# Gates and branch products of an encoder block computed with tokens on the partitions

## The chip, the cores and the metric

The kernel runs on one NeuronCore of a Trainium2 chip. The metric is device time in microseconds of one execution, taken as the median over several runs. The engines have short names in the profile: PE is TensorE with its matmuls, PEld its loading of the stationary operand, DVE is VectorE, ACT is ScalarE, POOL is GpSimd, SP is SyncE, which only issues DMAs here.

## What is computed

One layer of a bidirectional encoder on 256 tokens with 2048 features. The input is normed and projected by `w_in`; two attention branches (8 heads in a window, 12 dilated heads whose three groups merge to 4) give `ya` and `yb`; each is projected to 2048 features, multiplied with its gate and summed; an output projection, a gated MLP with a width-3 convolution over the tokens, and a gated embedding follow.

```python
for i in range(DEPTH):
    h = rms_norm(x, attn_norm[i])
    proj = h @ w_in[i]
    qa, ka, va, qb, kb, vb, ga, gb = jnp.split(proj, split_points, axis=-1)
    ya = windowed_gqa(qa, ka, va, rel_bias_table, sink_a[i])
    yb = dilated_attention(qb, kb, vb, rel_bias_table)
    merged = jax.nn.sigmoid(ga) * (ya @ w_branch_a[i]) + jax.nn.sigmoid(gb) * (yb @ w_branch_b[i])
    x = x + merged @ w_out[i]
    hf = rms_norm(x, ffn_norm[i])
    g = dwconv_centred(hf @ w_ffn_gate[i], conv_w[i], conv_b[i])
    x = x + (jax.nn.gelu(g) * (hf @ w_ffn_up[i])) @ w_ffn_down[i]
    gate_p = jax.nn.sigmoid(rms_norm(x, ple_norm[i]) @ w_ple_gate[i])
    x = x + gate_p * (p[i] @ w_ple_proj[i])
return rms_norm(x, final_norm)
```

The widths that matter: D_MODEL 2048 (16 blocks of 128), `ya` 1024 wide (8 blocks), `yb` 512 wide (4 blocks), the MLP 5632 wide (44 blocks). All inputs are float32.

## The kernel before

**Work.** All weights are cut into blocks of 128x128 and laid out in HBM in the order of use, in pieces of 16 blocks (1 MB). There are 4128 blocks. SyncE loads the pieces in turn into three buffers (`raw`, line 176). Every float32 operand is split into a high part that TensorE reads in one pass and the low rest: for each eight blocks, ScalarE copies the high part (`whi`, line 192) and VectorE subtracts it from the original (`wlo`, line 193). `split_to` issues that up to three groups of eight ahead; there are four buffers of each. A product is then high x high + high x low + low x high.

**Jobs.** `_plan` makes a list of jobs; the main loop (line 674 on) goes through it, and TensorE's instructions stand in that order. There are two forms.

- A *product job* (`product`, `block`) makes one output block of 128 features x 256 tokens, features on the partitions. Per weight block: the high weights are stationary and 512 columns move (256 tokens high, 256 tokens low, line 203); then the low weights are stationary and the 256 high columns move (line 204). `gather` adds the two 256-column halves of the accumulator (ScalarE line 254, VectorE line 258). The kinds are q, k, ga, gb, ba, bb, g and u.
- A *wide job* (`wide_product`) makes 256 tokens x 512 features, tokens on the partitions, in two accumulators of 128 tokens. Per step of four weight blocks and per half of the tokens, three matmuls of 512 columns: token block high with high weights, token block high with low weights, token block low with high weights (lines 226 to 228). The token block is stationary and the weights move. The kinds are v, o, d0, d1, pp and pg. Two of the v jobs take every second token (`TWINS`, a stationary operand with a step of two columns), for the dilated heads; the others take unbroken halves.

Each job of 16 blocks (a product job) or 64 blocks (a wide one over 2048 features) is followed by what other engines do with the result (`after`, `joined`, `gate`). Other pieces of work are put into the stream by `at((job, step), f)`: `run_due` calls f just before that step of that job. The last attention head group is handled so: scores one job later at step 9, the transposes of the softmax two jobs later at step 12, the product with the values three jobs later at step 4 (`attend`).

**The stage in question.** Job numbers 38 to 101 are ga n, gb n (gates, 16 blocks each, moving operand `hs`, the gained input) and ba n, bb n (branch products, 8 and 4 blocks, moving operand `yab`), for n = 0 to 15: 704 blocks. ga and gb are multiplied with the norm's factor and go through tanh (lines 574 to 577); a sigmoid is (tanh of half + 1)/2. ba and bb multiply (lines 580 to 588), and `halves` writes block n of `merged`, high and low part, features on the partitions, as o needs it for its stationary operand. In job o the tokens stand on the partitions; `joined` adds the residual `res`, and `flip` turns four columns of 128 back by four transposes on TensorE per call (line 618). `res` lies in the place of `x`, whose rows are fetched again from HBM by eight DMAs on ScalarE's queue (`fetch`, line 662), during ga 2 to ga 9.

**Places in SBUF.** The pools give every tile a fixed byte address per partition. Modulo 512, all `whi` and `wlo` buffers and both buffers named `mov` (which hold `hs`, then `merged`, `hf`, `pl`) are at 160; `yab` is at 0; `act` (the stationary operand of d0 and d1) and `pw` (that of pp) are at 96. The rows and halves inside these tiles are multiples of 512 bytes.

Of the kernel before, what the change touches and what calls it, by code (L numbers as in the profile page):

```python
# [10 lines left out]
F32 = mybir.dt.float32  # L11
# [5 lines left out]
P = 128  # L17
# [44 lines left out]
def _plan():  # L62
# [25 lines left out]
    lead = 2  # L88
    for n in range(KC + lead):
        if n < KC:  # L90
            jobs.append(("ga", n, "w_in", GA + n, 0, KC))
            jobs.append(("gb", n, "w_in", GB + n, 0, KC))
        if n >= lead:
            jobs.append(("ba", n - lead, "w_branch_a", n - lead, 0, QH))
            jobs.append(("bb", n - lead, "w_branch_b", n - lead, 0, HG))
    def wide(kind, name, k0, count):
        for c in range(QUARTERS):
            jobs.append((kind, c, name, tuple(range(4 * c, 4 * c + 4)), k0, count))

    wide("o", "w_out", 0, KC)  # L100
# [35 lines left out]
def _encoder(ctx: ExitStack, tc, xt, xrows, pt, cols, table, onehot, mask, ident_in, last_gain, wts, out):  # L136
# [187 lines left out]
    def at(i, f, *a):  # L324

        due.setdefault(i, []).append((f, a))
# [8 lines left out]
    yab = ap_.tile([P, QH + HG, 2 * T], FR, name="yab", bufs=1)  # L335
# [184 lines left out]
    def after(job, i, acc, u=None):  # L520
# [52 lines left out]
        elif kind in ("ga", "gb"):  # L573
            u = gather(acc)
            nc.vector.tensor_tensor(u, u, rt[0], op=ALU.mult)
            g = ap_.tile([P, T], F32, name="th", tag="k", bufs=7)
            nc.scalar.activation(g, u, AF.Tanh, scale=0.5)
            tg[kind, n] = g
        elif kind == "ba":
            u = gather(acc)  # L580
            m = ap_.tile([P, T], F32, name="ma", tag="q", bufs=4)
            nc.vector.scalar_tensor_tensor(m, tg.pop(("ga", n)), 1.0, u, op0=ALU.add, op1=ALU.mult)
            held["ma"] = m
        elif kind == "bb":
            u = gather(acc)
            m = ap_.tile([P, T], F32, name="mb", tag="q", bufs=4)
            nc.vector.scalar_tensor_tensor(m, tg.pop(("gb", n)), 1.0, u, op0=ALU.add, op1=ALU.mult)
            nc.vector.tensor_tensor(m, m, held["ma"], op=ALU.add)
            halves(held["merged"][:, n, :], m)
# [71 lines left out]
    def fetch(t, c):  # L661
# [3 lines left out]
        "q": lambda k: hs[:, k, :], "ba": lambda k: yab[:, k, :], "bb": lambda k: yab[:, QH + k, :],  # L665
        "g": lambda k: held["hf"][:, k, :],
    }
    for a in ("k", "ga", "gb"):
        movers[a] = movers["q"]
    movers["u"] = movers["g"]  # L670

    stills = {"o": "merged", "d0": "act", "d1": "act", "pp": "ps", "pg": "pl"}

    for i, job in enumerate(_JOBS):
        kind, n, _, _, _, blocks = job
        if kind == "ba" and n == 0:
# [22 lines left out]
        if kind == "ga" and 2 <= n < 10:  # L699
            at((i, 4), fetch, *divmod(n - 2, QUARTERS))  # L700
# [7 lines left out]
        if kind == "pp" and n == 2:  # L708
            half = held["half"] = held["ff"].tile([P, 2], F32, name="half")
            nc.vector.tensor_scalar(half, root(rowsums(held["ss2"]), 2), 0.5, None, op0=ALU.mult)  # L710
# [43 lines left out]
def _layout(inputs):  # L754
# [18 lines left out]
    for g, (window, dil) in enumerate(PATTERNS):  # L773
# [3 lines left out]
        "xt": xt, "xrows": np.asarray(inputs["x"])[0].reshape(2, P, D), "pt": pt, "cols": cols,  # L777
        "table": np.asarray(inputs["rel_bias_table"]), "onehot": onehot, "mask": mask, "ident": np.eye(P, dtype=f),
        "last_gain": np.broadcast_to(np.asarray(inputs["final_norm"]), (P, D)), "wts": wts.reshape(_NPIECES, P, PIECE * P),
    }  # L780
# [18 lines left out]
```

## Time and profile before

| | |
|---|---|
| median of 3 runs | 1500.01 us (1499.2 to 1501.3) |
| the profiled execution | 1501.29 us, span 1499.5 us |
| granted TensorE clock over the span | 0.996 |
| instructions in the trace | 20395, of them 7936 matmuls |
| read from HBM | 279.49 MB |

The span runs from the first to the last instruction of the profiled execution; the execution's own time has 1.8 us more around it. Busy times are shares of the span. Matmuls overlap each other in the trace (the next begins while the one before drains), so the mean duration of a matmul is longer than the distance between two of them; the distance is found from a stretch's length and the number of blocks in it. A view named "windows" gives such stretches. A line of the waits has the waiting engine and line, who released it, the time in total, the number of waits and the longest.

### The profile page before, as it was taken

The page shows a single profiled execution, that of the slowest core. Times are in us where ns is not written, and L with a number is a line of the kernel's source. Part 1 is how long each engine was busy: PE and PEld are TensorE (multiplying, and loading weights), DVE is VectorE, ACT ScalarE, POOL GpSimd, SP SyncE. Part 2 cuts the span into 40 slices and gives each one's busy share as a digit, 9 for nine tenths or more (in the row PEclk, how much of TensorE's full clock was granted, in tenths as well). Part 3 has the DMA queues.
Part 4 walks back from the last instruction along what each step waited for, and adds up shares of the span by engine and source line. Part 5 has one row for each costly group of instructions (what it writes and reads, how often), then busy time and mean ns, then how long its engine had stood idle before and what let it go on. Part 6 is the DMA issues. An engine that isn't in the chain of part 4 may idle for free.

```text
span 1499.5 us, 20395 instructions
## 1 busy us (share of the span) xinstructions
PE 1483.9 (99%) x7936; PEld 1276.7 (85%) x7936; DVE 1015.7 (68%) x1533; ACT 748.9 (50%) x1119; POOL 3.7 (0%) x9
## 2 busy tenths in 40 slices
PE   9999999999999999999999999999999999999997
PEld 8888888888888888888888888888888888888886
DVE  6596665666676675578888885447887877555565
ACT  6465444445555555555555554334554554444553
POOL 0000000000000000000000000000000000000000
PEclk9999999999999999999999999999999999999999
DMA  8744444445555554555554455444544545454452
GB/s 302 278 169 159 169 169 172 173 165 193 196 182 186 196 189 184 195 202 191 197 193 180 190 196 196 186 185 191 196 176 190 187 180 195 186 181 195 184 189 104
DMA packets 46380, 282.94 MB, mean 189 GB/s; under 512 B 5124, under 2 KB 9988, under 8 KB 14028
## 3 DMA queue, kind: packets, MB, share of 16 engines
q1 hardware_dynamic: 44268, 277.31, 50.0%
q10 hardware_dynamic: 2016, 4.33, 0.9%
q8 instruction: 62, 1.02, 0.3%
q14 instruction: 34, 0.28, 0.0%
HBM read 279.49 MB, written 2.14 MB: 188 GB/s over the span
## 4 chain that ended last, share of the span: by engine, by line
PE 95%; DMA 3%; DVE 1%; ACT 1%; issue 0%; SPq 0%; POOL 0%; POOLq 0%; DVEq 0%; ACTq 0%
PE acc L203 39%; PE acc L204 20%; PE acc L226 11%; PE acc L227 11%; PE acc L228 11%; DMA raw<-in_wts 2%; DMA x<-in_xrows 1%; PE pt L482 0%; PE pt L618 0%; DVE wlo L193 0%; PE misc L497 0%; PE sp L447 0%; PE misc L428 0%; PE misc L429 0%; PE misc L430 0%
## 5 line engine op out<-in xcount | busy, mean ns | idle before, releaser
L193 DVE TENSOR_TENSOR wlo<-raw,whi 128x1024 fp32r<-128x1024 f32 (+1 forms) x519 | 632.1, 1218 | 442.6 <-ACT whi L192 442.1
L192 ACT ACTIVATE whi<-raw 128x1024 fp32r<-128x1024 f32 (+1 forms) x519 | 547.7, 1056 | 666.5 <-PE acc L203 270.8
L203 PE MATMUL acc<-mov,whi 128*128 128x512 f32 x2352 | 826.5, 395 | 0.0
L204 PE MATMUL acc<-mov,wlo 128*128 128x256 f32 x2352 | 658.9, 280 | 0.0
L203 PEld LDWEIGHTS acc<-mov,whi 128*128 128x128 f32 x2352 | 440.8, 187 | 100.9
L204 PEld LDWEIGHTS acc<-mov,wlo 128*128 128x128 f32 x2352 | 444.3, 189 | 0.5
L226 PE MATMUL acc<-whi,mov 128*128 128x512 f32 (+1 forms) x384 | 148.6, 387 | 3.6 <-DVE first L258 3.6
L228 PE MATMUL acc<-whi,mov 128*128 128x512 f32 (+1 forms) x384 | 147.7, 385 | 0.0
L227 PE MATMUL acc<-wlo,mov 128*128 128x512 f32 (+1 forms) x384 | 147.6, 384 | 0.0
L226 PE MATMUL acc<-whi,act 128*128 128x512 f32 x352 | 138.6, 394 | 0.0
L227 PE MATMUL acc<-wlo,act 128*128 128x512 f32 x352 | 138.4, 393 | 0.0
L228 PE MATMUL acc<-whi,act 128*128 128x512 f32 x352 | 136.8, 389 | 0.0
L226 PEld LDWEIGHTS acc<-whi,mov 128*128 128x128 f32 x384 | 73.9, 193 | 18.0 <-DVE first L258 4.5
L228 PEld LDWEIGHTS acc<-whi,mov 128*128 128x128 f32 x384 | 73.8, 192 | 14.1
L227 PEld LDWEIGHTS acc<-wlo,mov 128*128 128x128 f32 x384 | 73.9, 192 | 13.2
L226 PEld LDWEIGHTS acc<-whi,act 128*128 128x128 f32 x352 | 66.1, 188 | 14.9
L228 PEld LDWEIGHTS acc<-whi,act 128*128 128x128 f32 x352 | 66.1, 188 | 14.9
L227 PEld LDWEIGHTS acc<-wlo,act 128*128 128x128 f32 x352 | 66.2, 188 | 13.1
L254 ACT ACTIVATE t<-acc 128x256 f32<-128x256 f32 x179 | 65.1, 368 | 8.9 <-PE acc L204 8.9
L203 PE MATMUL acc<-yab,whi 128*128 128x512 f32 x192 | 68.4, 395 | 0.0
L258 DVE TENSOR_TENSOR u<-acc,t 128x256 f32<-128x256 f32 x164 | 67.8, 417 | 0.0
L204 PE MATMUL acc<-yab,wlo 128*128 128x256 f32 x192 | 53.9, 280 | 0.0
(140 smaller groups left out, 906.5 us busy)
## 6 DMA issues: line engine op xcount, KB each, us to landing
raw<-in_wts SPq DMA_DIRECT2D x251, 1024.0 KB, 4.8
raw<-in_wts SPq DMA_DIRECT2D x12, 512.0 KB, 6.7
x<-in_xrows ACTq DMA_DIRECT2D x8, 256.0 KB, 6.5
x<-in_xt SPq DMA_DIRECT2D x13, 128.0 KB, 5.3
mov<-hold SPq DMA_DIRECT2D x3, 514.0 KB, 6.9
mov<-hold SPq DMA_DIRECT2D x2, 768.0 KB, 7.8
mov<-in_last_gain ACTq DMA_DIRECT2D x1, 1024.0 KB, 5.0
out<-x ACTq DMA_DIRECT2D x2, 384.0 KB, 3.5
```

The lines of the kernel that those rows point to most:

```text
L192: nc.scalar.activation(hi, src, AF.Copy)
L193: nc.vector.tensor_tensor(lo, src, hi.bitcast(F32), op=ALU.subtract)
L203: nc.tensor.matmul(acc, hi[:, o, :], m, start=first, stop=False, skip_group_check=True)
L204: nc.tensor.matmul(acc[:, T:], lo[:, o, :], m[:, :T], start=False, stop=last, skip_group_check=True)
L226: nc.tensor.matmul(acc, xh, hi, start=(k == 0), stop=False)
L227: nc.tensor.matmul(acc, xh, lo, start=False, stop=False)
L228: nc.tensor.matmul(acc, xl, hi, start=False, stop=(k == n - 1))
L254: keep(nc.scalar.activation(t, acc[:, T:], AF.Copy, scale=scale))
L258: nc.vector.tensor_tensor(u, acc[:, :T], t, op=ALU.add)
```

## The change

The stage ga, gb, ba, bb becomes wide jobs: for each quarter c of the output features the jobs ga c, gb c (64 blocks each), ba c (32) and bb c (16) follow each other. `hs` and the two parts of `yab` are now stationary, and the accumulators hold tokens on the partitions. ScalarE takes tanh straight from the accumulator with the norm's factor as its scale per partition; VectorE multiplies and adds from the accumulators (`gated`). The sum m of a quarter, 256 tokens x 512 features, is then turned by eight transposes on TensorE in two groups of four (`merge`), at steps 3 and 6 of the job after bb, which is the next ga, or o 0 for the last quarter. ScalarE and VectorE write the high and low part of `merged` from there. TensorE has 1056 matmuls of 512 columns and 32 transposes in this stage in place of 704 of 512 and 704 of 256 columns.

The last head's scores, transposes and value product move to steps 3, 8 and 11 of job ga 0. The eight fetches of the residual's rows move to step 6 of each ga and gb. The rows are declared after the weights among the kernel's inputs.

Places: `yab` gets 128 columns more and begins 160 bytes into its tile. The three tiles of row sums and the tile of half the norm's factor become one tile (`marks`). By this `yab`, `act` and `pw` all begin at 160 modulo 512.

```diff
-    lead = 2
-    for n in range(KC + lead):
-        if n < KC:
-            jobs.append(("ga", n, "w_in", GA + n, 0, KC))
-            jobs.append(("gb", n, "w_in", GB + n, 0, KC))
-        if n >= lead:
-            jobs.append(("ba", n - lead, "w_branch_a", n - lead, 0, QH))
-            jobs.append(("bb", n - lead, "w_branch_b", n - lead, 0, HG))
-    def wide(kind, name, k0, count):
-        for c in range(QUARTERS):
-            jobs.append((kind, c, name, tuple(range(4 * c, 4 * c + 4)), k0, count))
-
+    def wide(kind, name, k0, count, first=0, quarters=range(QUARTERS)):
+        for c in quarters:
+            n = first + 4 * c
+            jobs.append((kind, c, name, tuple(range(n, n + 4)), k0, count))
+
+    for c in range(QUARTERS):
+        wide("ga", "w_in", 0, KC, GA, [c])
+        wide("gb", "w_in", 0, KC, GB, [c])
+        wide("ba", "w_branch_a", 0, QH, 0, [c])
+        wide("bb", "w_branch_b", 0, HG, 0, [c])
...
-def _encoder(ctx: ExitStack, tc, xt, xrows, pt, cols, table, onehot, mask, ident_in, last_gain, wts, out):
+def _encoder(ctx: ExitStack, tc, xt, pt, cols, table, onehot, mask, ident_in, last_gain, wts, xrows, out):
...
-    yab = ap_.tile([P, QH + HG, 2 * T], FR, name="yab", bufs=1)
+    yab = ap_.tile([P, (QH + HG) * 2 * T + P], FR, name="yab", bufs=1)
+    yab = yab[:, 40:40 + (QH + HG) * 2 * T].rearrange("p (k t) -> p k t", t=2 * T)
...
-                at((i + 3, 4), values, w, heads, y)
-            at((i + 2, 11 if len(heads) == 1 else 12), second)
-        at((i + 1, 9), first)
+                at((i + 1, 11) if end else (i + 3, 4), values, w, heads, y)
+            at((i + 1, 8) if end else (i + 2, 11 if len(heads) == 1 else 12), second)
+        end = y == QH + HG - 1
+        at((i + 1, 3 if end else 9), first)
...
+    def gated(kind, n, t, acc):
+
+        th, m = held["th"], held["m"][:, t, :]
+        if kind in ("ga", "gb"):
+            nc.scalar.activation(th[:, kind == "gb", t, :], acc, AF.Tanh, scale=held["rc"][:, t:t + 1])
+        elif kind == "ba":
+            nc.vector.scalar_tensor_tensor(m, th[:, 0, t, :], 1.0, acc, op0=ALU.add, op1=ALU.mult)
+        else:
+            u = th[:, 1, t, :]
+            nc.vector.scalar_tensor_tensor(u, u, 1.0, acc, op0=ALU.add, op1=ALU.mult)
+            nc.vector.tensor_tensor(m, m, u, op=ALU.add)
+
+    def merge(n, e, m):
+
+        p = ps.tile([P, 2, T], F32, name="pt", bufs=2)
+        for c in range(2):
+            for t in range(2):
+                nc.tensor.transpose(p[:, c, t * P:(t + 1) * P], m[:, t, (2 * e + c) * P:(2 * e + c + 1) * P], ident)
+        k = 4 * n + 2 * e
+        hi, lo = (held["merged"][:, k:k + 2, c:c + T] for c in (0, T))
+        nc.scalar.activation(hi, p, AF.Copy)
+        nc.vector.tensor_tensor(lo, p, hi.bitcast(F32), op=ALU.subtract)
...
+    held.update(hs=hs, ya=yab[:, :QH, :], yb=yab[:, QH:, :])
+    stills = {"ga": "hs", "gb": "hs", "ba": "ya", "bb": "yb", "o": "merged", "d0": "act", "d1": "act", "pp": "ps", "pg": "pl"}
...
+        if kind == "ga" and n == 0:
+            held["rc"] = sc.tile([P, 2], F32, name="sum")
+            nc.vector.tensor_scalar(held["rc"], rc[0][:, :2], 0.5, None, op0=ALU.mult)
+        if kind == "gb" and n == 0:
...
-            for a in ("ss1", "ss2", "ss3"):
-                held[a] = ff.tile([P, 2, QUARTERS], F32, name=a)
+            marks = ff.tile([P, 5, 2, QUARTERS], F32, name="marks")
+            for e, a in enumerate(("ss1", "ss2", "ss3")):
+                held[a] = marks[:, e]
+            held["half"] = marks[:, 3, 0, :2]
...
-        if kind == "ga" and 2 <= n < 10:
-            at((i, 4), fetch, *divmod(n - 2, QUARTERS))
+        if kind in ("ga", "gb"):
+            at((i, 6), fetch, int(kind == "gb"), n)
+        if kind == "bb":
+            for e in range(2):
+                at((i + 1, 3 + 3 * e), merge, n, e, held["m"])
...
-            tag = ("pt" if kind == "pg" and n % 2 == 0 else "acc" if kind == "pg" else ("acc", "sp")[n % 2])
+            tag = ("pt" if kind == "pg" and n % 2 == 0 else "acc" if kind == "pg" else ("acc", "sp")[kind in ("gb", "bb") or kind not in ("ga", "ba") and n % 2])
...
+        elif kind in ("ga", "gb", "ba", "bb"):
+            if kind == "ga":
+                held["th"] = ap_.tile([P, 2, 2, W4], F32, name="th", tag="v", bufs=1)
+                held["m"] = ap_.tile([P, 2, W4], F32, name="m", tag="vf", bufs=1)
+            for t in range(2):
+                if t:
+                    rest()
+                gated(kind, n, t, acc[t])
```

More of the change, by code (lines that the diff above doesn't have):

```diff
@@ L572, in after @@
                 attend(i, [(QH + g * HG + j, KVH + g * HG + j) for g in range(NG)], QH + j)
[L573 to L589, printed above, removed]
         elif kind == "g":
@@ L664, in _encoder @@
     movers = {
-        "q": lambda k: hs[:, k, :], "ba": lambda k: yab[:, k, :], "bb": lambda k: yab[:, QH + k, :],
-        "g": lambda k: held["hf"][:, k, :],
-    }
-    for a in ("k", "ga", "gb"):
-        movers[a] = movers["q"]
+        "q": lambda k: hs[:, k, :], "g": lambda k: held["hf"][:, k, :],
+    }
+    movers["k"] = movers["q"]
     movers["u"] = movers["g"]
-    stills = {"o": "merged", "d0": "act", "d1": "act", "pp": "ps", "pg": "pl"}
+    held.update(hs=hs, ya=yab[:, :QH, :], yb=yab[:, QH:, :])
+    stills = {"ga": "hs", "gb": "hs", "ba": "ya", "bb": "yb", "o": "merged", "d0": "act", "d1": "act", "pp": "ps", "pg": "pl"}
     for i, job in enumerate(_JOBS):
         kind, n, _, _, _, blocks = job
-        if kind == "ba" and n == 0:
+        if kind == "ga" and n == 0:
+            held["rc"] = sc.tile([P, 2], F32, name="sum")
+            nc.vector.tensor_scalar(held["rc"], rc[0][:, :2], 0.5, None, op0=ALU.mult)
+        if kind == "gb" and n == 0:
             held["merged"] = big.tile([P, KC, 2 * T], FR, name="mov")
@@ L708, in _encoder @@
         if kind == "pp" and n == 2:
-            half = held["half"] = held["ff"].tile([P, 2], F32, name="half")
-            nc.vector.tensor_scalar(half, root(rowsums(held["ss2"]), 2), 0.5, None, op0=ALU.mult)
+            nc.vector.tensor_scalar(held["half"], root(rowsums(held["ss2"]), 2), 0.5, None, op0=ALU.mult)
         if i < FIRST:
@@ L776, in _layout @@
     return {
-        "xt": xt, "xrows": np.asarray(inputs["x"])[0].reshape(2, P, D), "pt": pt, "cols": cols,
+        "xt": xt, "pt": pt, "cols": cols,
         "table": np.asarray(inputs["rel_bias_table"]), "onehot": onehot, "mask": mask, "ident": np.eye(P, dtype=f),
         "last_gain": np.broadcast_to(np.asarray(inputs["final_norm"]), (P, D)), "wts": wts.reshape(_NPIECES, P, PIECE * P),
+        "xrows": np.asarray(inputs["x"])[0].reshape(2, P, D),
     }
```

## The prediction

> **What bounds the kernel now.** I read the page's busy shares and chain first, then TensorE's waits, then a table by stage. The page:
>
> ```profile
> PE 1483.9 (99%) x7936; PEld 1276.7 (85%) x7936; DVE 1015.7 (68%) x1533; ACT 748.9 (50%) x1119; POOL 3.7 (0%) x9
> PEclk9999999999999999999999999999999999999999
> PE 95%; DMA 3%; DVE 1%; ACT 1%; issue 0%; SPq 0%; POOL 0%; POOLq 0%; DVEq 0%; ACTq 0%
> ```
>
> TensorE is busy for 99% of the span at full clock and is 95% of the chain that ended last. The view of its waits adds up to under 6 us:
>
> ```profile
> PE acc L226 <- DVE first L258: 3.6, 1, 3.6
> PE misc L159 <- DVE mhalf L154: 1.1, 1, 1.1
> PE first L203 <- DVE mov L271: 0.9, 1, 0.9
> PE first L203 <- ACT whi L192: 0.2, 1, 0.2
> ```
>
> All of it lies in the start; behind it no other engine holds TensorE up. So the change can pay only by the number of matmuls and by the pace at which they follow each other. The pace is read from stretches that begin and end with a job (columns: stretch, its length, busy time and instructions of TensorE, then the same of the others, granted clock, DMA share, GB/s):
>
> ```profile
> core 0: us, PE busy (x) PEld busy (x) DVE busy (x) ACT busy (x) POOL busy (x), PEclk, DMA share, GB/s
> 153.83:178.01 24.18, 24.18 (x119) 20.34 (x118) 14.90 (x19) 10.96 (x15) 0.00 (x0) 1.00 0.44 153
> 235.22:257.62 22.40, 22.40 (x98) 18.53 (x97) 10.77 (x10) 9.26 (x10) 0.00 (x0) 1.00 0.48 169
> 312.48:349.98 37.50, 37.50 (x231) 33.30 (x229) 24.13 (x34) 18.75 (x30) 0.00 (x0) 1.00 0.45 168
> 349.98:562.08 212.10, 212.10 (x1218) 186.07 (x1217) 145.28 (x220) 112.24 (x176) 0.00 (x0) 1.00 0.51 188
> 562.08:583.88 21.80, 21.80 (x98) 18.03 (x97) 13.15 (x18) 9.97 (x13) 0.00 (x0) 1.00 0.54 205
> 583.88:606.64 22.76, 22.76 (x106) 18.80 (x104) 12.78 (x15) 11.47 (x16) 0.00 (x0) 1.00 0.49 177
> 664.64:897.62 232.98, 232.98 (x1347) 205.43 (x1346) 192.59 (x343) 120.60 (x191) 0.00 (x0) 1.00 0.53 192
> 897.62:1018.46 120.84, 120.84 (x531) 99.14 (x529) 59.71 (x57) 47.22 (x46) 0.00 (x0) 1.00 0.50 190
> 1024.10:1267.18 243.08, 243.08 (x1378) 210.82 (x1377) 195.95 (x346) 122.77 (x194) 0.00 (x0) 1.00 0.50 186
> 1402.63:1467.90 65.27, 65.27 (x290) 54.04 (x289) 36.86 (x37) 31.73 (x39) 0.00 (x0) 1.00 0.53 195
> ```
>
> (Two or three matmuls under way at an edge are counted too.) I divide each by its weight blocks of 128x128. Both forms stream 768 columns a block: a product job 512+256, a wide job six matmuls of 512 for four blocks.
> - Product jobs: u 0 to u 21 (664.64 on, 42 jobs of 16 blocks) 232.98/672 = 346.7 ns a block; g 23 to u 43 (1024.10 on, 43 jobs) 243.08/688 = 353.3 ns. Same lines, same tiles: two paces.
> - Wide jobs: pg 0 to 2 (1402.63 on) 65.27/192 = 340.0 ns; o 0 (562.08) 21.80/64 = 340.6; d0 (897.62) 120.84/352 = 343.3; the fourth v job (235.22), whose stationary takes every second column, 22.40/64 = 350.0.
>
> The kernel's pools put the weight halves and both mov tiles (hs, merged, hf, pl) at bytes that are 160 modulo 512; act, d0's stationary, is at 96. That is the one difference I find between 340.0 and 343.3.
>
> **The change, part by part.** I sum on the profiled execution: span 1499.5 us, time 1501.3 with 1.8 us around it, 1.3 us over the median of 1500.0. What is saved I take from the median.
>
> *The gate stage* (ga, gb, ba, bb) now takes 37.50 + 212.10 = 249.6 us for 704 blocks, with 36 matmuls of the last attention head in its first 37.5 us: 37.50 - 96 x 0.3467 = 4.2 us for those. Afterwards the 704 blocks are wide jobs. With hs and yab at 160 modulo 512, I take pg's 340.0 ns: 239.4 us. Bounds: 340.0 (pg) and 350.0 (the fourth v job), 7.0 us apart. I take the low end since o and pg have the same shape and place, and since the third v job (153.83), which reads the same hs as unbroken 128 columns, is 24.18 us with 20 foreign matmuls inside; at 350.0 its 64 blocks would be 22.4 and leave 1.8 us, under the 0.11 to 0.12 us each that such ones take below. The head's 36 matmuls stay: 4.2.
>
> *Added:* 32 transposes in groups of four. The o jobs hold the same thing: o 1 with eight transposes is 22.76 against 21.80 for o 0, so 0.96 us per quarter; three fall into the stage, one into o 0: 3.8 us. Stage and o 0: 239.4 + 4.2 + 3.8 = 247.4, against 249.6: **-2.2 us**.
>
> *Operands' place:* act and pw move from 96 to 160 modulo 512. d0 at pg's pace is 352 x 0.340 = 119.7 against 120.84: -1.2; d1, of the same shape: -1.2; pp, 32 blocks: -0.1. **-2.4 us**; bounds 0 and -2.4, and I take the full value because pg and o stand exactly there.
>
> Sum -4.6: span 1494.9, median **1495.4 us**.
>
> One rule weighs against the d0 term: the Trainium skill ("TensorE: Matmul & The Clock Gate", Part 2) says that loading the next stationary tile takes no SBUF read bandwidth from the running matmul, as each has its own port; by it the place would not matter and the sum would be -2.2. The 343.3 against 340.0 ns of this trace speaks against it.
>
> *Removed from the other engines:* 64 gathers, 32 multiplications, the tanh, the products with the gates.
>
> ```profile
> L193 DVE TENSOR_TENSOR wlo<-raw,whi 128x1024 fp32r<-128x1024 f32 x514 | 629.1, 1224 | 439.4 <-ACT whi L192 438.9
> L192 ACT ACTIVATE whi<-raw 128x1024 fp32r<-128x1024 f32 x514 | 545.1, 1061 | 665.6 <-PE acc L203 270.8 <-PE acc L228 236.8 <-issue 137.5
> L258 DVE TENSOR_TENSOR u<-acc,t 128x256 f32<-128x256 f32 x164 | 67.8, 417 | 0.0
> L254 ACT ACTIVATE t<-acc 128x256 f32<-128x256 f32 x179 | 65.1, 368 | 8.9 <-PE acc L204 8.9
> L575 DVE TENSOR_TENSOR u<-u,rms 128x256 f32<-128x256 f32 x32 | 13.6, 425 | 1.1
> L638 DVE SCALAR_TENSOR_TENSOR gate<-gate,ph 128x512 f32<-128x512 f32 x8 | 5.5, 692 | 6.3 <-ACT gate L637 6.3
> L487 DVE TENSOR_TENSOR near<-pt,near 128x512 fp32r<-128x512 f32 x12 | 8.2, 685 | 0.4 <-ACT near L486 0.3
> ```
>
> On VectorE alone 64 x 0.417 + 32 x 0.425 = 40 us go and eight operations of 0.69 us a quarter come (22 us). None of it is on TensorE's path, so I cost it at nothing; the cover is TensorE's own 99%.
>
> *The new waits.* A quarter's first transpose waits for both halves of m, and behind it in TensorE's queue stands the whole next job. It is due three steps, 3 x 4 x 0.340 = 4.1 us, after bb ends. VectorE's order there is as in the o stage:
>
> ```profile
> 582.46 1.23 DVE L193 TENSOR_TENSOR wlo<-raw,whi 128x1024 fp32r<-128x1024 f32 x1 [1.49 <-ACT whi L192]
> 583.61 1.28 DVE L628 SCALAR_TENSOR_TENSOR x<-acc,x 128x512 f32<-128x512 f32 x2
> 585.19 1.22 DVE L193 TENSOR_TENSOR wlo<-raw,whi 128x1024 fp32r<-128x1024 f32 x1 [0.30 <-ACT whi L192]
> ```
>
> The job's operations begin 0.3 us before its end (583.88) with no split ahead of them. Four of 0.69 us are done 2.5 us after bb ends, 1.6 us early: no wait. If one split slips in (1.22 us) there is still none; with two and ScalarE's 1.06 it is 1.9 us a quarter. The last head's pieces move from product steps to wide steps:
>
> ```profile
> 315.65 0.28 PE L428 MATMUL sp<-kf,qf 128*128 128x256 f32 x1
> 315.77 0.28 PE L429 MATMUL sp<-kf,qf 128*128 128x256 f32 x1
> 322.48 0.88 DVE L470 TENSOR_SCALAR s<-s,rd 128x512 f32<-128x512 f32 x2
> 323.86 0.60 PE L482 MATMUL pt<-ident,s 128*128 128x128 f32 x4
> ```
>
> Scores at 315.65 have their softmax done at 323.36, 7.7 us later. Afterwards the transposes follow the scores by five wide steps, 6.8 us, and the scores' own 14 matmuls, 1.6: 8.4 us. That covers it by 0.7 us; without the cover it costs under 1 us, once.
>
> *The rows' fetch*, the same eight DMAs from ScalarE's queue:
>
> ```profile
> x<-in_xrows ACTq DMA_DIRECT2D x8, 256.0 KB, 6.5
> ```
>
> They start at step 6 of each ga and gb. The last lands 6.5 us after its issue and is used over 30 us later, after gb 3, ba 3, bb 3 and o 0. Declaring xrows last changes an address in HBM and no instruction: 0. The shared tile for the row sums and one VectorE multiplication of two columns: 0.
>
> **The rivals.** *The place does nothing:* d0 and d1 stay at 343.3 and only the gate stage gains, 1497.8 us. For it: each tile is the only sample of its place. Against it: pg and o agree to 0.6 ns in two different tiles.
>
> *The first u/g pass changes pace.* Product jobs go at 346.7 or 353.3 ns and keep to one until something else comes between:
>
> ```profile
> 652.13:655.31 3.18, 3.18 (x20) 2.76 (x19) 3.15 (x5) 1.79 (x3) 0.00 (x0) 1.00 0.91 322
> 661.78 0.59 PE L306 MATMUL misc<-rdg,ones 128*128 128x256 f32 x2
> 1018.46:1024.10 5.64, 5.64 (x34) 4.90 (x32) 3.42 (x4) 2.12 (x2) 0.00 (x0) 1.00 0.54 203
> ```
>
> The first nine blocks of g 0, behind o 3, go at 3.18/9 = 353.3; after two groups of transposes and the norm's broadcast (661.78) the pace is 346.7 from u 0 on. Should this hand-over come out otherwise, 704 blocks x 6.6 ns = 4.7 us come back: 1500.1. Against it: g 0 and g 1 hold the same instructions behind the same o 3. *The second pass changes pace* the other way, since the d0 before it runs differently: 1490.7. Against it: behind d0 (1018.46, g 22, 5.64/16 = 352.5) as behind o 3, whose pace d0 would take on, the slower pace comes first, and nothing comes between later.
>
> *The slower side: columns set the pace.* If TensorE is paid by the streamed column, 768 a block in both forms and wherever the operands lie, the gate stage stays at what its blocks cost now ((249.6 - 4.2)/704 = 348.6 ns) and the transposes come on top: 1500.0 + 3.8 = 1503.8. It decides from the gate stage's pace: with no gain in d0 the change loses above 343.2 ns a block, with it above 346.6. For it: the fourth v job is wide and at 350.0. Against it: o and pg. The same section of the Trainium skill's TensorE page ("Back-to-back issue gap") gives N/2.4 + 2.5 ns for an isolated matmul; my estimate from it is 325.0 ns a product block and 323.7 a wide one, 0.9 us in all, so the sum would be 3.8 - 0.9 = +2.9 us. The trace's 340.0 against 346.7 does not agree with it.
>
> **How the numbers follow.** Forecast 0.66, place does nothing 0.10, first pass slower 0.09, second pass faster 0.06, columns 0.09. Time 1495.4, the likeliest's own range 1493.4 to 1497.5 (a wait or two at the transposes, d0 in part). The range 1493.0 to 1500.6 takes in the first three, 0.85. A change under 0.2% (3.0 us, from 1497.0 to 1503.0) cannot be told from none. Faster: nine tenths of the forecast and the second pass, 0.66; same: the rest of the forecast, the place and the first pass, 0.25; slower: 0.09.
>
> **What would show it.** In the changed profile: wide groups on hs and yab at 680 ns per three matmuls of a half (340.0 a block); d0's four jobs in 119.7 us, not 120.84; u 0 to u 21 still 233.0 and g 23 to u 43 still 243.1; no wait of TensorE on m. Wrong would be a gate stage with o 0 over 271 us together, transposes that wait for VectorE, or u/g passes with other lengths.

## The result, and the profile after

The changed kernel takes 1495.53 us (median of 7 runs, 1494.23 to 1496.85), the kernel before 1500.38 us on the same chip (7 runs, 1496.65 to 1501.30). The ratio is 0.9967 with a 95% interval from 0.9957 to 0.9977, so 3.5 to 6.5 us are saved. The forecast was 1495.4. In a second set of 12 runs the same kernel took 1496.62 us, so an agreement to 0.1 us is more than one set of runs can promise. The profiled execution took 1494.23 us, its span 1492.4.

The page of the changed kernel (busy times, chain) and its view of TensorE's waits:

```profile
PE 1478.4 (99%) x7616; PEld 1261.6 (85%) x7616; DVE 976.3 (65%) x1406; ACT 728.3 (49%) x1031; POOL 3.7 (0%) x9
PE 95%; DMA 2%; DVE 1%; ACT 1%; issue 0%; SPq 0%; POOL 0%; ACTq 0%; POOLq 0%; DVEq 0%
```

```profile
PE acc L224 <- DVE first L256: 2.4, 1, 2.4
PE misc L157 <- DVE mhalf L152: 1.1, 1, 1.1
PE first L201 <- ACT whi L190: 0.6, 1, 0.6
PE first L201 <- DVE mov L269: 0.2, 1, 0.2
```

TensorE has 320 matmuls less and is the bound as before. The waits are the same four kinds in the start; none names m (L615) or a transpose of it (L622). VectorE's 39 us and ScalarE's 21 us of work that went away bought nothing, as they lay beside a TensorE that is busy for 99%.

The table by stretch, cut at starts of jobs, with the prediction's columns. First the changed kernel (v 0 starts at 49.60, ga 0 at 310.05, gb 1 at 396.77, ba 1 at 418.54, ga 2 at 434.86, o 0 at 556.40, g 0 at 647.33, u 0 at 659.85, d0 0 at 892.81, g 22 at 1012.53, g 23 at 1018.17, d1 0 at 1261.26, pp 0 at 1383.80):

```profile
core 0: us, PE busy (x) PEld busy (x) DVE busy (x) ACT busy (x) POOL busy (x), PEclk, DMA share, GB/s
49.60:310.05 260.45, 260.36 (x1495) 228.89 (x1496) 176.01 (x276) 131.27 (x216) 1.02 (x1) 0.99 0.48 180
310.05:556.40 246.35, 246.35 (x1118) 204.66 (x1117) 129.40 (x127) 109.72 (x118) 0.00 (x0) 1.00 0.51 188
396.77:418.54 21.77, 21.77 (x98) 18.03 (x97) 9.80 (x8) 9.75 (x11) 0.00 (x0) 1.00 0.51 193
418.54:434.86 16.32, 16.32 (x74) 13.52 (x73) 8.75 (x9) 7.14 (x8) 0.00 (x0) 1.00 0.55 194
556.40:647.33 90.93, 90.93 (x417) 75.21 (x416) 51.71 (x59) 45.40 (x62) 0.00 (x0) 1.00 0.50 188
659.85:892.81 232.96, 232.96 (x1347) 205.41 (x1346) 192.26 (x343) 120.81 (x191) 0.00 (x0) 1.00 0.51 193
892.81:1012.53 119.72, 119.72 (x531) 99.10 (x529) 59.61 (x57) 47.26 (x46) 0.00 (x0) 1.00 0.51 193
1018.17:1261.26 243.09, 243.09 (x1379) 210.72 (x1378) 196.08 (x346) 122.79 (x194) 0.00 (x0) 1.00 0.50 187
1261.26:1383.80 122.54, 122.54 (x555) 101.52 (x554) 64.85 (x68) 56.00 (x70) 0.00 (x0) 1.00 0.50 188
1383.80:1492.40 108.60, 98.96 (x441) 81.66 (x439) 61.25 (x74) 54.43 (x75) 1.80 (x3) 0.98 0.43 159
```

The stretches of the kernel before that were not shown yet, at the same jobs (v 0, o 0 to o 3, d1, and pp with what follows):

```profile
51.00:312.48 261.48, 261.38 (x1495) 230.02 (x1496) 175.99 (x275) 131.29 (x216) 1.02 (x1) 0.99 0.49 180
562.08:652.13 90.05, 90.05 (x410) 74.42 (x409) 50.73 (x60) 45.06 (x63) 0.00 (x0) 1.00 0.52 189
1267.18:1390.70 123.52, 123.52 (x554) 101.51 (x553) 64.84 (x68) 56.06 (x70) 0.00 (x0) 1.00 0.50 187
1390.70:1499.50 108.80, 99.11 (x441) 81.68 (x439) 61.32 (x74) 54.40 (x75) 1.80 (x3) 0.97 0.43 159
```

| stretch | before | after | difference | forecast |
|---|---|---|---|---|
| start, up to v 0 | 51.00 | 49.60 | -1.40 | 0 |
| v 0 up to the gate stage | 261.48 | 260.45 | -1.03 | 0 |
| gate stage and o | 339.65 | 337.28 | -2.37 | -2.2 |
| u 0 to u 21 | 232.98 | 232.96 | 0.0 | 0 |
| d0 | 120.84 | 119.72 | -1.12 | -1.2 |
| g 23 to u 43 | 243.08 | 243.09 | 0.0 | 0 |
| d1 | 123.52 | 122.54 | -0.98 | -1.2 |
| pp and the rest | 108.80 | 108.60 | -0.20 | -0.1 |

Behind the start of the gate stage the spans differ by 4.7 us; the sum of the forecast was 4.6. The 2.4 us ahead of that say nothing of the change. 1.4 us lie in the start, where the first weights arrive: over the profiled executions of this study v 0 begins anywhere from 49.1 to 54.2 us, and at 54.2 in a second profile of the very same changed kernel. The other 1.0 us lie between v 0 and the gate stage, which the change leaves alone; that stretch lasts 260.1 to 261.4 us over the same executions, whichever the kernel. The edges at pp 0 are rounded by some hundredths: from its first matmul to that of pp 0, d1 lasts 123.54 us before and 122.50 after, so it gains 1.04, and what follows gains about 0.1.

What the reader is to see in the stage itself: gb 1 takes 21.77 us for 64 blocks, ba 1 and bb 1 together 16.32 for 48, which is 340.2 and 340.0 ns a block. Now the first quarter's turn, and the head's softmax, in the timeline of the changed kernel (start, duration, engine, line, operation; the bracket is idle time before it):

```profile
314.14 0.28 PE L427 MATMUL sp<-kf,qf 128*128 128x256 f32 x1
320.02 0.88 DVE L469 TENSOR_SCALAR s<-s,rd 128x512 f32<-128x512 f32 x2
322.56 1.03 PE L481 MATMUL pt<-ident,s 128*128 128x128 f32 x8
373.80 1.28 DVE L614 SCALAR_TENSOR_TENSOR th<-th,acc 128x512 f32<-128x512 f32 x2
374.08 0.39 PE L224 MATMUL acc<-whi,mov 128*128 128x512 f32 x1
374.99 1.28 DVE L615 TENSOR_TENSOR m<-m,th 128x512 f32<-128x512 f32 x2
376.20 1.22 DVE L191 TENSOR_TENSOR wlo<-raw,whi 128x1024 fp32r<-128x1024 f32 x1
378.17 0.60 PE L622 MATMUL pt<-ident,m 128*128 128x128 f32 x4
```

bb 0 ends and ga 1 begins at 374.08. m is done at 374.99 + 1.28 = 376.27, 2.2 us later (forecast 2.5), and the transposes come at 378.17, 4.1 us later as forecast: 1.9 us to spare. No split of weights slips in between. The softmax is done at 320.90 and its transposes come at 322.56, with 1.7 us to spare where 0.7 were counted on.

### The profile page after: what moved, and what is told of

Same layout as the page of the kernel before. It is cut to its first block, busy times and chain, and to the rows that moved or that the text cites. A ratio compares the mean times of both kernels' runs of the same rounds, so it can differ in the third digit from the quotient of the medians.

```text
span 1492.4 us, 19451 instructions
## 1 busy us (share of the span) xinstructions
PE 1478.4 (99%) x7616; PEld 1261.6 (85%) x7616; DVE 976.3 (65%) x1406; ACT 728.3 (49%) x1031; POOL 3.7 (0%) x9
## 4 chain that ended last, share of the span: by engine, by line
PE 95%; DMA 2%; DVE 1%; ACT 1%; issue 0%; SPq 0%; POOL 0%; ACTq 0%; POOLq 0%; DVEq 0%
PE acc L201 28%; PE acc L224 17%; PE acc L225 17%; PE acc L226 16%; PE acc L202 14%; DMA raw<-in_wts 2%; PE pt L481 0%; PE pt L601 0%; DMA x<-in_xrows 0%; DVE wlo L191 0%; ACT whi L190 0%; PE misc L496 0%; PE sp L446 0%; PE pt L622 0%; PE misc L427 0%
## 5 line engine op out<-in xcount | busy, mean ns | idle before, releaser
L190 ACT ACTIVATE whi<-raw 128x1024 fp32r<-128x1024 f32 (+1 forms) x519 | 547.6, 1056 | 683.2 <-PE acc L226 356.3
L201 PE MATMUL acc<-mov,whi 128*128 128x512 f32 x1840 | 647.9, 396 | 0.0
L202 PE MATMUL acc<-mov,wlo 128*128 128x256 f32 x1840 | 515.6, 280 | 0.0
L201 PEld LDWEIGHTS acc<-mov,whi 128*128 128x128 f32 x1840 | 345.0, 188 | 79.9
L202 PEld LDWEIGHTS acc<-mov,wlo 128*128 128x128 f32 x1840 | 347.7, 189 | 0.5
L224 PE MATMUL acc<-whi,mov 128*128 128x512 f32 (+1 forms) x640 | 248.6, 388 | 2.4 <-DVE first L256 2.4
L225 PE MATMUL acc<-wlo,mov 128*128 128x512 f32 (+1 forms) x640 | 246.8, 386 | 0.0
L226 PE MATMUL acc<-whi,mov 128*128 128x512 f32 (+1 forms) x640 | 246.8, 386 | 0.0
L224 PEld LDWEIGHTS acc<-whi,mov 128*128 128x128 f32 x640 | 121.4, 190 | 26.4 <-DVE first L256 3.3
L226 PEld LDWEIGHTS acc<-whi,mov 128*128 128x128 f32 x640 | 121.4, 190 | 24.0
L225 PEld LDWEIGHTS acc<-wlo,mov 128*128 128x128 f32 x640 | 121.5, 190 | 23.0
L201 PE MATMUL first<-mov,whi 128*128 128x512 f32 x112 | 39.2, 401 | 0.8 <-ACT whi L190 0.6
L226 PE MATMUL acc<-whi,yab 128*128 128x512 f32 x96 | 37.3, 389 | 0.0
```

Source lines behind the costliest of these rows:

```text
L190: nc.scalar.activation(hi, src, AF.Copy)
L201: nc.tensor.matmul(acc, hi[:, o, :], m, start=first, stop=False, skip_group_check=True)
L202: nc.tensor.matmul(acc[:, T:], lo[:, o, :], m[:, :T], start=False, stop=last, skip_group_check=True)
L224: nc.tensor.matmul(acc, xh, hi, start=(k == 0), stop=False)
L225: nc.tensor.matmul(acc, xh, lo, start=False, stop=False)
L226: nc.tensor.matmul(acc, xl, hi, start=False, stop=(k == n - 1))
```

## The experiments

Each starts from the changed kernel unless it says otherwise. "Place" means the byte address in a partition. The weights' buffers lie at 160 modulo 256, so an operand at 160 has the distance 0 from them.

### Which operand's place is worth what

*act and pw back at 96 modulo 512.* The shared tile for the row sums goes away again.

```diff
-            marks = ff.tile([P, 5, 2, QUARTERS], F32, name="marks")
-            for e, a in enumerate(("ss1", "ss2", "ss3")):
-                held[a] = marks[:, e]
-            held["half"] = marks[:, 3, 0, :2]
+            for a in ("ss1", "ss2", "ss3"):
+                held[a] = ff.tile([P, 2, QUARTERS], F32, name=a)
...
```

> The changed kernel with act and pw back at byte 96 modulo 512 (the row sums and half the norm's factor in tiles of their own). Place theory: the four d0 jobs take 120.84 us again in place of 119.76, d1 gives back 1.1 us as well, pp 0.1; everything else as in the changed kernel, gate stage 246.4 us; time 2.3 us over the changed kernel's 1495.5, so 1497.8. Rival, the place does nothing and d0 gained from what runs before it: d0 stays at 119.76, time 1495.5.

1498.74 us (10 runs), ratio to before 0.999 with the interval 0.998 to 0.9999. The rows of d0, and of d1 (which is cut a digit coarser):

```profile
895.13:1015.98 120.85, 120.85 (x530) 99.16 (x529) 59.70 (x57) 47.22 (x46) 0.00 (x0) 1.00 0.53 191
1264.70:1388.30 123.60, 123.60 (x555) 101.56 (x554) 64.91 (x68) 56.06 (x70) 0.00 (x0) 1.00 0.53 186
```

Both are back at the length of before (120.84 and, between the first matmuls, 123.54), while the gate stage keeps its gain (246.3 us, 312.4 to 558.7). The time is 0.9 us over the 1497.8 that was expected; v 0 begins at 51.3 us in this profile and at 49.6 in that of the changed kernel, a difference within the scatter of the start.

*The same the other way: before, with only act and pw moved.*

```diff
-            for a in ("ss1", "ss2", "ss3"):
-                held[a] = ff.tile([P, 2, QUARTERS], F32, name=a)
+            marks = ff.tile([P, 5, 2, QUARTERS], F32, name="marks")
+            for e, a in enumerate(("ss1", "ss2", "ss3")):
+                held[a] = marks[:, e]
+            held["half"] = marks[:, 3, 0, :2]
...
```

> The kernel before with nothing but act and pw moved from byte 96 to 160 modulo 512. Place theory: d0 119.7 us in place of 120.84, d1 gains 1.1 us, pp 0.1, the gate stage stays at 249.6 us; time 2.3 us under before's 1500.4: 1498.1. Rival, the place does nothing without the new stage: d0 stays at 120.84 and the time at 1500.4.

1497.63 us (10 runs), ratio 0.9987 (0.9977 to 0.9996). d0, and d1:

```profile
896.59:1016.31 119.72, 119.72 (x530) 99.11 (x529) 59.62 (x57) 47.26 (x46) 0.00 (x0) 1.00 0.54 193
1265.00:1387.50 122.50, 122.50 (x554) 101.52 (x553) 64.82 (x69) 56.02 (x70) 0.00 (x0) 1.00 0.52 189
```

With no instruction of the gate stage changed, d0 and d1 last 119.72 and 122.50 us, as in the changed kernel. So the gain in d0 and d1 comes and goes with this edit in both directions. The edit also moves the tiles behind act in its pool; that it is the place of act itself is shown by the eight places below, where only the reading of act moves.

*yab back at 0 modulo 512.*

```diff
-    yab = yab[:, 40:40 + (QH + HG) * 2 * T].rearrange("p (k t) -> p k t", t=2 * T)
+    yab = yab[:, :(QH + HG) * 2 * T].rearrange("p (k t) -> p k t", t=2 * T)
```

> The changed kernel with yab at byte 0 modulo 512, where it was, act and pw left at 160. Place theory: the ba and bb jobs (192 blocks, 10.88 and 5.44 us each now, 340.0 ns a block) become slower, by 0.1 us a ba job if place 0 costs what place 96 cost d0 (343.3 ns), by 0.3 us if it costs the 350.0 ns of the fourth v job; the sum over the stage is 0.6 to 1.9 us. Rival, the place does nothing: 10.88 and 5.44 us.

One time, 1497.5 us. gb 1, then ba 1 with bb 1:

```profile
398.30:420.06 21.76, 21.76 (x97) 18.02 (x96) 9.81 (x8) 9.74 (x11) 0.00 (x0) 1.00 0.54 194
420.06:436.92 16.86, 16.86 (x73) 13.56 (x72) 8.83 (x9) 7.14 (x8) 0.00 (x0) 1.00 0.54 188
```

gb, whose stationary hs is where it was, is unchanged; ba and bb go at 16.86/48 = 351.3 ns instead of 340.0. Over 192 blocks that is 2.2 us, more than the 0.6 to 1.9 that was expected. The stage and o 0 together then last 271.4 us (311.0 to 582.4), and before they lasted 271.4 too (312.48 to 583.88). So the rewrite into wide jobs by itself, with yab where it was, pays nothing here: what the wide pace saves in ga and gb, the transposes and the slow ba and bb take back. Nearly all of the 4.6 us hangs on the operands' place: 2.3 us on that of act and pw, 2.2 us on that of yab. What moving yab would bring in the old form was not tried. There ba and bb were already slower than ga and gb: in the kernel before, ba 6 and bb 6 take 4.24 us for 12 blocks (442.02 to 446.26), 353.3 ns each, and ga 8 and gb 8 ahead of them 11.10 us for 32 (430.92 to 442.02), 346.9. Whether yab's place made that difference is not shown.

### The place by itself

*Eight places for act.* act gets room, and each of the eight jobs d0 and d1 reads it at another shift; the two dilated v jobs read unbroken halves instead of every second token. The MLP's product and the dilated values so differ from the reference's; TensorE's instructions are of the same number and shape.

```diff
...
-            acc, _ = wide_product(i, hs, blocks, len(n), "acc", TWINS if far else HALVES)
+            acc, _ = wide_product(i, hs, blocks, len(n), "acc", HALVES)
...
+            if kind in ("d0", "d1"):
+                s = (0, 8, 16, 24, 32, 64, 96, 112)[4 * (kind == "d1") + n]
+                still = held["room"][:, s:s + FHALF * 2 * T].rearrange("p (k t) -> p k t", t=2 * T)
...
```

> The changed kernel whose d0 and d1 jobs read act from eight shifted places: shifts of 0, 32, 64, 96 bytes in d0 0 to 3 and 128, 256, 384, 448 in d1 0 to 3 (the columns are shifted with them, so the MLP's product is another one), and the two dilated v jobs read unbroken halves of hs in place of every second token (other values too). Place theory: 29.92 us at shift 0, 30.21 (d1: 31.1 with its transposes, against 30.84) at shift 448, which is byte 96 modulo 512; a shift by 128, 256 or 384 bytes tells whether the pace goes by the address modulo 128, 256 or 512: 29.92 and 30.84 again if it does. The fourth v job, without the step of two columns, 21.76 us in place of 22.40. Rival, the place does nothing: all eight jobs alike. Rival for v: hs's use and not the step makes 350 ns, then 22.40 stays.

One time, 1493.59 us, in which the second u/g pass is at the faster pace (below). The rows are the fourth v job, d0 at shifts of 0, 32, 64 and 96 bytes, then d1 at 128, 256, 384 and 448 (the last three of d1 hold eight transposes each):

```profile
232.92:254.71 21.79, 21.79 (x99) 18.03 (x98) 10.77 (x10) 9.24 (x10) 0.00 (x0) 1.00 0.49 170
892.31:922.28 29.97, 29.97 (x135) 24.77 (x133) 15.60 (x18) 12.24 (x13) 0.00 (x0) 1.00 0.52 191
922.28:953.07 30.79, 30.79 (x134) 24.80 (x132) 14.74 (x14) 11.66 (x11) 0.00 (x0) 1.00 0.53 191
953.07:983.87 30.80, 30.80 (x134) 24.82 (x132) 14.70 (x14) 11.66 (x11) 0.00 (x0) 1.00 0.52 184
983.87:1014.78 30.91, 30.91 (x133) 24.86 (x132) 14.68 (x14) 11.68 (x11) 0.00 (x0) 1.00 0.54 191
1258.84:1289.52 30.68, 30.68 (x135) 24.87 (x133) 15.66 (x18) 12.24 (x13) 0.00 (x0) 1.00 0.51 186
1289.52:1320.37 30.85, 30.85 (x142) 25.56 (x140) 16.37 (x18) 14.60 (x19) 0.00 (x0) 1.00 0.55 189
1320.37:1351.91 31.54, 31.54 (x141) 25.65 (x140) 16.48 (x18) 14.68 (x19) 0.00 (x0) 1.00 0.50 183
1351.91:1383.04 31.13, 31.13 (x141) 25.58 (x140) 16.40 (x18) 14.63 (x19) 0.00 (x0) 1.00 0.53 188
```

Divided by 88 blocks: 340.6 ns at 0, 349.9 at 32, 350.0 at 64, 351.3 at 96, 348.6 at 128. At 256 the job takes 30.85 us, as the changed kernel's d1 1 to d1 3 do at 0 ((122.54 - 29.98)/3 = 30.85, with 29.98 for d1 0). At 384 it is 0.69 longer than that, and at 128 it was 0.71 longer than at 0; at 448 it is 0.28 longer, where act stood before. So in both pairs, 0 and 256, 128 and 384, the pace repeats after 256 bytes. The 351.3 at 96 agrees with ba and bb above: yab at 0 is 96 past 160, modulo 256. The data read here differ with the shift too; in the experiments that move all of yab or act they do not. The fourth v job takes 21.79 us with unbroken halves and took 22.40 with a step of two columns: that step costs 9.5 ns a block.

*All of them moved together.* A tiny tile ahead of the weights' buffers gets 96 bytes more.

```diff
-    warm = const.tile([P, 4], F32, name="warm")
+    warm = const.tile([P, 28], F32, name="warm")[:, :4]
```

> The changed kernel with 96 bytes more in a small tile ahead of the weights' buffers, so that weights, hs, merged, hf, pl, yab, act and pw all move by 96 bytes together: from 160 to 0 modulo 256 bytes. Nothing else changes. Theory A (only the distance between stationary and moving operand counts): every pace stays, gb 1 in 21.76 us, ba 0 in 10.88, d0 1 in 29.92, u 0 to u 21 in 233.0, and the time is that of the changed kernel, 1495.5 to 1496.7 us. Theory B (the address itself counts, and 160 modulo 256 is the good one): the wide jobs go at the 350 to 351 ns that yab and act had at other addresses, gb 1 in 22.4 us, d0 1 in 30.8, some 2200 wide blocks x 10 ns = 22 us slower, about 1518 us.

1501.55 us (10 runs), ratio 1.001 (1.0001 to 1.002). The rows are gb 1, ba 1 with bb 1, u 0 to u 21, and d0:

```profile
397.74:419.50 21.76, 21.76 (x98) 18.02 (x96) 9.80 (x8) 9.74 (x11) 0.00 (x0) 1.00 0.59 195
419.50:435.82 16.32, 16.32 (x74) 13.52 (x72) 8.75 (x9) 7.14 (x8) 0.00 (x0) 1.00 0.52 191
661.01:898.45 237.44, 237.44 (x1346) 205.85 (x1345) 192.81 (x343) 120.74 (x191) 0.00 (x0) 1.00 0.53 189
898.45:1018.20 119.75, 119.75 (x531) 99.11 (x529) 59.55 (x56) 47.26 (x46) 0.00 (x0) 1.00 0.54 192
```

The wide jobs keep 340.0 ns with everything at 0 modulo 256. So it is the distance between stationary and moving operand that counts, not the address, as far as two addresses can show it: theory A for the pace. Its time was missed all the same, by nearly 5 us, for another reason: u 0 to u 21 take 237.44 us instead of 232.96. The prediction's rival "the first u/g pass changes pace" happened here, at 4.5 us, where it was priced at 4.7; the rest of the miss was not traced. The tiles `ident` and `ones`, the constant operands of the transposes and of the norm's broadcast, stayed where they were while their partners moved; that this is why the broadcast in g 1 no longer hands over the fast pace is argued, not shown.

### The pace of the product passes

*The second pass at eleven places.* The moving operand hf is read shifted in all but the last of its 16 rows, four jobs per shift (0 to 256 bytes in steps of 32, then 384 and 448), so the MLP's second half has other values.

```diff
...
+    def shifted(k):
+        s = moved.get("by", 0) if k < KC - 1 else 0
+        return held["hf"].rearrange("p k t -> p (k t)")[:, k * 2 * T + s:(k + 1) * 2 * T + s]
...
-        "q": lambda k: hs[:, k, :], "g": lambda k: held["hf"][:, k, :],
+        "q": lambda k: hs[:, k, :], "g": shifted,
...
```

> The changed kernel whose second u/g pass reads its moving operand hf from shifted places, four jobs each: 0, 32, 64, 96, 128, 160, 192, 224, 256, 384 and 448 bytes (the columns are shifted with them in all but the last of 16 rows, so the MLP's product is another one). Theory that the place sets the pace of product jobs as it does that of wide ones, modulo 256 bytes: the four jobs at 256 bytes go like those at 0, the others up to 10 ns a block slower than 353.3; 340.0 ns, the pace of the wide jobs, may appear at some shift. Rival, a product job's pace is only the state handed over to it: 353.3 at every shift, 249.0 us for the pass.

One time, 1494.7 us. Shifts of 0, 32, 128 and 256 bytes:

```profile
1014.65:1037.26 22.61, 22.61 (x130) 19.59 (x128) 17.54 (x30) 10.83 (x16) 0.00 (x0) 1.00 0.54 193
1037.26:1059.49 22.23, 22.23 (x131) 19.64 (x129) 18.07 (x33) 11.41 (x18) 0.00 (x0) 1.00 0.52 188
1104.35:1126.78 22.43, 22.43 (x130) 19.66 (x129) 18.41 (x34) 11.40 (x18) 0.00 (x0) 1.00 0.51 186
1194.12:1216.74 22.62, 22.62 (x130) 19.60 (x129) 18.29 (x33) 11.41 (x18) 0.00 (x0) 1.00 0.49 185
```

Per block of the 64: 353.3 ns at 0 and at 256, 347.3 at 32, 350.5 at 128. The four jobs at 384 take 22.44 us, as at 128, and those at 448 take 22.56, where those at 192 take 22.54. The pace of product jobs depends on the place too, with the same period, so the rival of one pace at every shift is wrong. The expectation was wrong in another way: it had the other shifts slower than 0, and none is. No shift reaches the wide jobs' 340.0, and the pace at 0 is one of two that occur there.

*An extra broadcast early in the second pass.* In the first pass the fast pace comes behind the norm's broadcast in g 1. The same two matmuls, with a result that nobody uses, are put at step 9 of g 23.

```diff
...
+        if kind == "g" and n == FHALF + 1:
+            at((i, 9), lambda: held.update(again=spread(held["dg"])))
```

> The changed kernel with one more matmul, the broadcast of the norm as in g 1, at step 9 of g 23 in the second u/g pass; its result is not used. Theory that the product jobs' pace is a state that lasts until something comes between: from u 22 on the pass goes at 346.7 ns a block in place of 353.3, 42 jobs of 16 blocks gain 4.5 us, the matmul costs 0.5, time 1491.5. Rival, the second pass is slower for a reason of its own (its tiles, its loads): pace stays at 353.3, time 1496.0.

1493.30 us (5 runs), ratio 0.9948 (0.9934 to 0.9961). The same once more, beside the changed kernel itself on one chip:

> The broadcast at step 9 of g 23 once more, beside the changed kernel on one chip: second pass 244.6 us and 4.1 us under the changed kernel, as in its first profile; 1491.4.

> The changed kernel once more, unedited, to stand beside the next two on one chip: 1495.5 us within 1 us, second u/g pass from g 22 to d1 0 in 248.8 us.

1493.35 us with the broadcast (5 runs, ratio 0.9949, 0.9936 to 0.9963) and 1496.62 without (12 runs, ratio 0.9973, 0.9964 to 0.9981). With it, the rows are g 22, g 23, and u 22 to u 43:

```profile
1014.46:1020.10 5.64, 5.64 (x34) 4.90 (x32) 3.45 (x4) 2.12 (x2) 0.00 (x0) 1.00 0.57 206
1020.10:1026.14 6.04, 6.04 (x36) 5.27 (x35) 4.42 (x7) 2.70 (x4) 0.00 (x0) 1.00 0.55 212
1026.14:1259.10 232.96, 232.96 (x1346) 205.41 (x1345) 191.41 (x339) 120.22 (x191) 0.00 (x0) 1.00 0.52 189
```

and u 22 to u 43 of the changed kernel on that chip:

```profile
1028.92:1266.36 237.44, 237.44 (x1347) 205.91 (x1346) 191.77 (x340) 120.41 (x191) 0.00 (x0) 1.00 0.51 186
```

g 23 is 0.4 us longer, and the 42 jobs behind it run at 346.7 ns instead of 353.3, 4.5 us shorter; in the first profile of this edit u 22 to u 43 take 232.9 us as well. The two ratio intervals don't meet, though only just (0.9963 and 0.9964). Of the kernels here that compute the layer it is the fastest. The stretch came out as expected (244.6 us from g 22 on); both times are 1.8 to 2.0 us over the 1491.5 and 1491.4 expected. Beside the changed kernel on its chip it is 3.3 us shorter by the medians and 4.1 by the stretch.

*The broadcast a job earlier,* at step 2 of g 22:

```diff
...
+        if kind == "g" and n == FHALF:
+            at((i, 2), lambda: held.update(again=spread(held["dg"])))
```

> The changed kernel with the norm's broadcast matmul at step 2 of g 22, the first job of the second u/g pass, in place of step 9 of g 23. Theory that any broadcast inside a slow product job hands over the fast pace: g 23 is at 346.7 ns too, 0.15 us better than the broadcast in g 23, so second pass 244.5 us, time 1491.3. Rival, it depends on the step and the phase in which the broadcast comes: 353.3 stays, 1495.9.

1497.56 us (12 runs), ratio 0.998 (0.9971 to 0.9988); g 22, then u 22 to u 43:

```profile
1013.08:1019.15 6.07, 6.07 (x35) 5.27 (x34) 3.45 (x4) 2.12 (x2) 0.00 (x0) 1.00 0.60 217
1024.80:1262.24 237.44, 237.44 (x1347) 205.88 (x1345) 191.74 (x340) 120.40 (x191) 0.00 (x0) 1.00 0.51 186
```

A miss: the price is paid and the pace stays at 353.3. So a broadcast does not hand over the fast pace wherever it stands: one of the two points tried did, the other didn't. What makes a point right stays open.

### The waits and the rows

*The transposes three steps earlier.*

```diff
-                at((i + 1, 3 + 3 * e), merge, n, e, held["m"])
+                at((i + 1, 3 * e), merge, n, e, held["m"])
```

> The changed kernel with a quarter's two groups of transposes at steps 0 and 3 of the next job in place of 3 and 6. Step of the prediction (VectorE has m ready 2.5 us after bb, so step 3, at 4.1 us, waits for nothing): at step 0 TensorE waits about 2.5 us in each of four quarters, 10 us in all, time 1505; a wait by the first transpose on VectorE line 615. Rival, m is ready much earlier or only the first columns are awaited: under 1 us a quarter, time under 1499.

1495.62 us (6 runs), ratio 0.9969 (0.9958 to 0.998), no wait on m. The 1505 us that were expected were missed, and the wait was not tested: TensorE ran the first transpose not at the start of ga 1 (377.50) but 1.8 us behind it, at 379.32, and the other three of its group from 379.91 on, among the matmuls of the steps 1 and 2. m is done at 379.70; the first transpose reads only its first half. What a wait would cost stays open.

*The rows declared in their old place.*

```diff
-def _encoder(ctx: ExitStack, tc, xt, pt, cols, table, onehot, mask, ident_in, last_gain, wts, xrows, out):
+def _encoder(ctx: ExitStack, tc, xt, xrows, pt, cols, table, onehot, mask, ident_in, last_gain, wts, out):
```

> The changed kernel with the residual's rows declared second among the inputs again. My step (an address in HBM and no instruction, 0 us): gate stage 246.4, d0 119.8, and a time within 1 us of the changed kernel's 1495.5; the start, from the first instruction to job v 0, lies anywhere between the 49.6 us of the changed kernel's profile and the 51.0 of before's. Rival, the rows' place slows the loads of the start: about 2.5 us more, 1498, and a start of 51 us or more, since the gate stage begins at 310.0 us in the changed kernel's profile and at 312.5 in before's.

1496.08 us (7 runs), ratio 0.9972 (0.9961 to 0.9982), against 0.9967 for the changed kernel. The gate stage lasts 246.4 us (312.2 to 558.6), as in the changed kernel. v 0 begins at 51.9 us, within the scatter of 49.1 to 54.2. The order of the inputs is worth nothing that can be measured.

## Why the prediction was right

- **The bound.** Right: TensorE is busy for 99% after as before, and only the number and the pace of its matmuls moved the time. The 60 us of VectorE and ScalarE work that went away, and the eight fetches in their new places (5.9 us to landing), show up nowhere. The prediction's sum for VectorE, 40 us less and 22 more, was too small: it counted the 64 gathers and 32 multiplications and left out the operations of ba and bb and the low parts of merged, so 39 us of busy time went away on balance and not 18. As TensorE waits for none of it, the time does not change by that.
- **The gate stage.** Forecast 246.5 us without o 0, measured 246.35; with o -2.2, measured -2.37. The pace of 340.0 ns was read off pg and o, from tiles of the same shape and place, and it holds for hs and for yab. What the prediction didn't price apart is that 192 of these blocks have it only because yab was moved; left at 0 they cost 2.2 us, and the step would have come out at 0.
- **The operands' place.** Forecast -2.4, measured -1.12 in d0, -1.04 in d1 and about -0.1 behind it, so -2.3. d1 was taken as d0's twin at -1.2 and got a little less. The prediction had a single sample of each place, and its reading that the place makes the difference was a guess until then; the eight shifts and the two experiments that moved act there and back show it. The rule of the Trainium skill that it weighed ("TensorE: Matmul & The Clock Gate", Part 2: two independent read ports, so that loading the next stationary tile takes nothing from the running matmul) is not borne out as a statement on time: at equal instruction counts the same job takes 29.97 to 30.91 us by the stationary operand's place.
- **The transposes.** Forecast 0.96 us per quarter. ga 1 to ga 3 take 22.69 us against 21.76 for a job of the same length without them: 0.93.
- **The total.** That 1495.53 lies 0.1 us from the forecast is luck: the same kernel took 1496.62 us in the second set of runs, and starts differ by up to 5 us between single executions. What bears the forecast out is the stretches, each within 0.2 us.
- **The waits.** None came. m was done 0.3 us earlier than worked out, and the softmax had 1 us more to spare. How much a transpose that is due too early would cost was not measured.
- **The rivals.** "The place does nothing" fell with the experiments on act. "Columns set the pace" fell with 340.0 in all wide jobs at distance 0; its one support, the fourth v job at 350.0, is the step of two columns. The two rivals on the u/g passes didn't occur in this change, but both did in others: the first pass at 353.3 when all places moved by 96 bytes, the second at 346.7 with the extra broadcast, and also in the experiment with eight places, where d0 3 ahead of it read act 96 bytes off (1014.78 to 1258.84, 244.06 us from g 22 to d1). Which of that experiment's edits did it is not shown. The reason given against the first, that g 0 and g 1 hold the same instructions, held here; it is not enough in general, because in the moved kernel they hold the same instructions too.

## What to carry to other kernels

Where TensorE is the bound, compare the pace per weight block of all stages before thinking about other engines, and when two stages of equal shape differ, look at the byte addresses of the stationary and the moving operand: here their distance modulo 256 was worth 3% of ba and bb and 1% of d0 and d1, and some unused bytes in a tile put it right. A long run of alternating matmuls can sit in a slower pace until something else comes between; look for a stretch of the same code that goes faster, find what stands ahead of it, and try that, but measure, since the same insertion a job and a half ahead of the good place cost 0.4 us and gained nothing. An edit that only shifts addresses can flip such a pace and hide the gain under test, so read the stretches and not the total alone.

## What the runs showed that was not expected

- The distance of the two operands sets the pace of 128x512 matmuls with new weights each time: 340.0 ns per block at 0 and 256 bytes, 348.6 to 351.3 at 32, 64, 96 and 128, and 343.3 at 448, which is 192 modulo 256 (d0 of before). Moving both together by 96 bytes leaves 340.0. What in the chip causes it no run here shows.
- A stationary operand with a step of two columns costs 350.0 ns a block against 340.5 (22.40 and 21.79 us for 64 blocks).
- The product pairs of 512 and 256 columns have two paces at distance 0, 346.7 and 353.3 ns a block. A pass of 42 jobs keeps the one in which it begins, and a broadcast of two matmuls turned it at step 9 of g 23 and not at step 2 of g 22. The reason stays open.
